# Linear attention on one core: loading V directly into a block layout, with a 128-row first matmul

## Chip, cores, metric

One core of one Trainium2 chip. The metric is device time in microseconds (us) of one execution; most kernels were run several times, and the median is quoted. "Span" is the length of the profiled execution as the trace has it; the measured time is some 1.8 us longer than the span of the same run. Lower is better.

## The reference

```python
batch, heads, seq, dim = 8, 12, 512, 64          # Q, K, V: float32
Q_feat = np.maximum(0, Q) + 1
K_feat = np.maximum(0, K) + 1
KV = np.einsum('bhkd,bhkv->bhdv', K_feat, V)
K_sum = np.sum(K_feat, axis=2)
numerator   = np.einsum('bhqd,bhdv->bhqv', Q_feat, KV)
denominator = np.einsum('bhqd,bhd->bhq', Q_feat, K_sum)
return numerator / (denominator[:, :, :, None] + 1e-10)
```

There are 96 independent heads. Q, K, V and the result are 12.58 MB each. The kernels work in bf16 inside; the loads convert on the way.

## The kernel before

The 96 heads are worked off in 12 groups of 8 heads. A tile has 128 partitions; 32 partitions hold the rows of one head, and the index `n` of 2 picks one of two sets of four heads. So a group has four row blocks `b` of 32 partitions. Loads run four groups ahead (`IN_BUFS`), stores follow three groups behind (`LAG`).

```python
IN_BUFS = 4; OUT_BUFS = 7; LAG = 3
...
def load(g):
    ...
    (nc.sync if first else nc.gpsimd).dma_start(out=k_raw, in_=k_dram[:, g*2 : g*2+2])
    nc.gpsimd.dma_start(out=v_raw, in_=v_dram[:, g*2 : g*2+2])
    nc.gpsimd.dma_start(out=q_raw, in_=q_dram[:, g*2 : g*2+2])

def features(g):                       # max(x + 1, 1) on VectorE; V is copied beside a column of ones
    for half in range(2):
        feature(kf[...], k_raw[...])
        nc.scalar.copy(out=va[:, cs]...[:, :, :, 0:D], in_=v_raw[:, :, cs])     # L110
    ...                                # qf likewise
def kv_and_transpose(g):
    for c in range(16):
        for b in range(4):             # four row tiles of 32 rows, 130 columns each
            nc.tensor.matmul(kva_ps[b//2][:, b%2, 0:130],                       # L126
                lhsT=kf[32*b:32*b+32, c], rhs=va[32*b:32*b+32, c], ...)
    ...                                # PSUM -> kva (ScalarE), transposes of qf, copies to qt (ScalarE)
def output(g):                         # o = qt x kva, then divide by the last column (VectorE)
    ...
for g in range(NG - 1):
    features(g)
    if g >= 1: kv_and_transpose(g - 1)
    if g >= 2: output(g - 2)
    if g + IN_BUFS < NG: load(g + IN_BUFS)
    if g >= LAG: store(g - LAG)
...                                    # the last two groups, then the last four stores
```

All stores but the last go out from GpSimd; the last group's is cut in two halves, issued by SyncE.

## Time and profile before

| | before |
|---|---|
| time, median of 4 runs | 128.02 us (127.78 to 128.51) |
| span of the profiled run | 126.5 us |
| busy share: TensorE, VectorE, ScalarE | 53%, 45%, 51% |
| busy share of the 16 DMA engines, inner slices | 90% or more in each |
| transfers that GpSimd issues | 46 |

No compute engine is busy for much over half of the span, while the DMA engines never rest between the first and the last 3 us. The prediction shows the lines and reads them.

One more view is used in this text. The trace marks, for each transfer, the moments at which each of the 16 DMA engines had finished its share. "First" below is the first of these 16 marks, "last" the last; the transfer counts as landed at the last. Where all engines slip by the same time, both move; where one engine falls behind, only the last moves.

### The profile page before, as it was taken

The page shows a single profiled execution, that of the slowest core. Times are in us where ns is not written, and L with a number is a line of the kernel's source. Part 1 is how long each engine was busy: PE and PEld are TensorE (multiplying, and loading weights), DVE is VectorE, ACT ScalarE, POOL GpSimd, SP SyncE. Part 2 cuts the span into 40 slices and gives each one's busy share as a digit, 9 for nine tenths or more (in the row PEclk, how much of TensorE's full clock was granted, in tenths as well). Part 3 has the DMA queues.
Part 4 walks back from the last instruction along what each step waited for, and adds up shares of the span by engine and source line. Part 5 has one row for each costly group of instructions (what it writes and reads, how often), then busy time and mean ns, then how long its engine had stood idle before and what let it go on. Part 6 is the DMA issues. An engine that isn't in the chain of part 4 may idle for free.

```text
span 126.5 us, 3107 instructions
## 1 busy us (share of the span) xinstructions
PE 67.4 (53%) x1344; PEld 54.8 (43%) x1344; DVE 57.3 (45%) x144; ACT 64.1 (51%) x97; POOL 35.2 (28%) x56
## 2 busy tenths in 40 slices
PE   0009139147949486674648547737916972674000
PEld 0009028036838275562537435626714851563000
DVE  0122222058292865919377067147229079805500
ACT  4041095393966939397590492293096592073000
POOL 6992233222332242233223322332221202010000
PEclk9999999999995958679985555555555577569555
DMA  3999999999999999999999999999999999999990
GB/s 75 340 211 208 212 211 213 208 212 210 214 208 211 212 209 214 209 215 208 251 336 212 229 358 209 212 365 214 210 338 249 215 306 418 420 422 405 409 356 33
DMA packets 13341, 32.17 MB, mean 254 GB/s; under 512 B 784, under 2 KB 784, under 8 KB 13328
## 3 DMA queue, kind: packets, MB, share of 16 engines
q0 software_dynamic: 12512, 29.89, 99.9%
q1 hardware_dynamic: 816, 2.10, 4.6%
q8 instruction: 10, 0.16, 0.5%
q14 instruction: 3, 0.02, 0.0%
HBM read 37.75 MB, written 12.58 MB: 398 GB/s over the span
## 4 chain that ended last, share of the span: by engine, by line
DMA 61%; DVE 13%; PE 8%; POOL 5%; issue 3%; ACT 2%; ACTq 1%; POOLq 0%; DVEq 0%
DMA q_raw<-in_Q_dram 46%; DMA v_raw<-in_V_dram 15%; DVE o_sb L170 9%; PE kva_ps L126 5%; PE qt_ps L146 2%; DVE recip L169 2%; DVE qf L98 2%; POOL v_raw L84 1%; POOL q_raw L85 1%; ACT qt L147 1%; POOL k_raw L81 1%; ACTq L232 1%; ACT v_aug L110 1%; PE o_ps L159 1%; POOL kva_diag L186 1%
## 5 line engine op out<-in xcount | busy, mean ns | idle before, releaser
L110 ACT COPY v_aug<-v_raw 128x1024 bf16<-128x1024 bf16 x24 | 24.1, 1056 | 40.5 <-DMA v_raw<-in_V_dram 40.4
L159 PE MATMUL o_ps<-kva_diag,qt 128*64 128x130 bf16 x384 | 22.9, 269 | 26.7 <-ACT kva_diag L137 15.9
L126 PE MATMUL kva_ps<-v_aug,kf 32*128 32x130 bf16 x768 | 24.6, 294 | 22.8 <-ACT v_aug L110 13.0
L170 DVE TENSOR_TENSOR o_sb<-o_ps,recip 128x512 f32<-128x512 f32 x48 | 33.2, 691 | 1.7
L126 PEld LDWEIGHTS <-kf 32*128 32x128 bf16 x768 | 19.7, 132 | 26.9 <-issue 14.6
L159 PEld LDWEIGHTS <-qt 128*64 128x64 bf16 x384 | 16.6, 137 | 32.7 <-issue 19.1
L147 ACT COPY qt<-qt_ps 128x1024 bf16<-128x1024 bf16 x24 | 29.5, 1298 | 0.5
L98 DVE TENSOR_SCALAR qf<-q_raw 128x1024 bf16<-128x1024 bf16 x24 | 9.4, 434 | 39.0 <-DMA q_raw<-in_Q_dram 39.0
L146 PE MATMUL qt_ps<-identity,qf 128*128 128x128 bf16 x192 | 21.4, 301 | 0.0
L146 PEld LDWEIGHTS <-qf 128*128 128x128 bf16 x192 | 18.5, 140 | 2.3 <-issue 2.0
L92 POOL DMA_DIRECT2D out_dram<-o_sb x11 | 8.4, 767 | 27.9 <-DVE o_sb L170 13.6
L98 DVE TENSOR_SCALAR kf<-k_raw 128x1024 bf16<-128x1024 bf16 (+1 forms) x24 | 9.7, 446 | 12.2 <-DMA k_raw<-in_K_dram 12.2
L137 ACT CAST kva_diag<-kva_ps 64x130 bf16<-64x130 f32 x48 | 10.2, 262 | 9.1 <-PE kva_ps L126 8.8
L169 DVE RECIPROCAL recip<-o_ps 128x8 f32<-128x8 f32 x48 | 9.5, 197 | 8.7 <-PE o_ps L159 8.7
L84 POOL DMA_DIRECT2D v_raw<-in_V_dram x12 | 8.7, 726 | 16.8 <-ACT kva_diag L137 7.3
L85 POOL DMA_DIRECT2D q_raw<-in_Q_dram x12 | 8.6, 720 | 15.8 <-DMA q_raw<-in_Q_dram 5.3
L81 POOL DMA_DIRECT2D k_raw<-in_K_dram x11 | 7.9, 714 | 15.4 <-DMA v_raw<-in_V_dram 8.2
L110 ACT ACT_TABLE_LOAD x1 | 1.3, 1283 | 0.7 <-PEq L221 0.7
L186 POOL MEMSET kva_diag<- 128x520 bf16 x2 | 1.0, 528 | 0.0
L188 POOL MEMSET v_aug<- 128x32 bf16 x2 | 0.4, 278 | 0.0
masks.py:199 POOL TENSOR_SCALAR_AFFINE_SELECT identity<-identity 128x128 bf16<-128x128 bf16 x1 | 0.3, 288 | 0.1
masks.py:197 POOL MEMSET identity<- 128x128 bf16 x1 | 0.2, 232 | 0.0
(4 smaller groups left out, 0.4 us busy)
## 6 DMA issues: line engine op xcount, KB each, us to landing
out_dram<-o_sb POOLq DMA_DIRECT2D x11, 1024.0 KB, 19.9
v_raw<-in_V_dram POOLq DMA_DIRECT2D x12, 512.0 KB, 19.4
q_raw<-in_Q_dram POOLq DMA_DIRECT2D x12, 512.0 KB, 19.4
k_raw<-in_K_dram POOLq DMA_DIRECT2D x11, 512.0 KB, 19.4
k_raw<-in_K_dram SPq DMA_DIRECT2D x1, 1024.0 KB, 4.9
out_dram<-o_sb SPq DMA_DIRECT2D x2, 512.0 KB, 6.9
```

Source lines behind the costliest of these rows:

```text
L81: (nc.sync if first else nc.gpsimd).dma_start(out=k_raw, in_=k_dram[:, g * 2 : g * 2 + 2])
L84: nc.gpsimd.dma_start(out=v_raw, in_=v_dram[:, g * 2 : g * 2 + 2])
L85: nc.gpsimd.dma_start(out=q_raw, in_=q_dram[:, g * 2 : g * 2 + 2])
L98: nc.vector.tensor_scalar(out=dst, in0=src, scalar1=1.0, scalar2=1.0, op0=ALU.add, op1=ALU.max)
L110: nc.scalar.copy(out=va[:, cs].rearrange("p c (n x) -> p n c x", n=2)[:, :, :, 0:D], in_=v_raw[:, :, cs],)
L126: nc.tensor.matmul(kva_ps[b // 2][:, b % 2, 0:W], lhsT=kf[ps, c, :, :], rhs=va[ps, c, :], start=(c == 0), stop=(c == C2 - 1),)
L137: nc.scalar.copy(out=kva[ps, 2 * h : 2 * h + 2, n, :], in_=kva_ps[h][ps, :, D1 * n : D1 * n + D1],)
L146: nc.tensor.transpose(qt_ps[:, c, :], qf[:, half * C + c, :, :], identity)
L147: nc.scalar.copy(out=qt[:, :, :, half], in_=qt_ps)
L159: nc.tensor.matmul(ops[c // 4][64 * j : 64 * j + 64, c // 2 % 2, (c % 2) * W : (c % 2) * W + W], lhsT=qt[:, c, 32 * b : 32 * b + 32, :], r ...
L169: nc.vector.reciprocal(out=recip, in_=cells[:, :, :, :, D:D1])
L170: nc.vector.tensor_tensor(out=o_sb[:, h:NP:2, 4 * i : 4 * i + 4].rearrange("p n (b c) d -> p b c n d", b=2), in0=cells[:, :, :, :, 0:D], i ...
```

## The change

Intent: take the copy of V off ScalarE and use the full height of the array in the first matmul. V is loaded straight into a tile with five blocks per partition; a partition's V goes into the block of its own head, the other three head blocks stay zero, and the fifth holds ones that give the sum of K. One matmul over 128 rows then serves four heads. As the block depends on the partition, a load of V becomes four loads of 32 partitions. The buffers are zeroed once by VectorE. The program order changes too: loads run three groups ahead instead of four, and the first matmul of a group follows directly on the output of two groups earlier. It gets two PSUM buffers of its own, and the pool shared before goes from three buffers to two.

```diff
-OUT_BUFS = 7
+OUT_BUFS = 6
+AHEAD = 3
...
-    v_aug = [const.tile([P, C2, W], BF16, ...) for i in range(2)]
+    v_blk = [const.tile([P, 5, 2, C2, D], BF16, ...) for i in range(3)]
...  load(g)
-        nc.gpsimd.dma_start(out=v_raw, in_=v_dram[:, g * 2 : g * 2 + 2])
-        nc.gpsimd.dma_start(out=q_raw, in_=q_dram[:, g * 2 : g * 2 + 2])
+        if first: (load q_raw here)
+        for b in range(4):
+            nc.gpsimd.dma_start(
+                out=v_blk[g % NV][32 * b : 32 * b + 32, b],
+                in_=v_dram[32 * b : 32 * b + 32, 2 * g : 2 * g + 2])
+        if not first: (load q_raw here)
...  features(g): the ScalarE copy of V is gone
...  first matmul
-        for c in range(C2):
-            for b in range(4):
-                nc.tensor.matmul(kva_ps[b // 2][:, b % 2, 0:W], lhsT=kf[ps, c], rhs=va[ps, c, :], ...)
+        for c in range(C2):
+            for n in range(2):
+                nc.tensor.matmul(kva_ps[64 * n : 64 * n + 64],
+                    lhsT=kf[:, c, n, :], rhs=vb[:, :, n, c, :], ...)      # 320 columns
...  start of the program
+        nc.vector.memset(ones, 0.0)
+        for t in v_blk:    nc.vector.memset(t, 0.0)
+        for t in kva_diag: nc.vector.memset(t, 0.0)
...  main loop
-        for g in range(IN_BUFS): load(g)
+        for g in range(AHEAD): load(g)
...
-            if g >= 1: kv_and_transpose(g - 1)
+            if g >= 1: transposes(g - 1)
             if g >= 2: output(g - 2)
-            if g + IN_BUFS < NG: load(g + IN_BUFS)
+            keys_values(g)
+            if g + AHEAD < NG: load(g + AHEAD)
```

## The prediction

> **What bounds the kernel now.** I read the page first for the DMA row, then the DMA queues, then the waits, then the timelines of the engines around the last load and at the end.
>
> ```profile
> DMA  3999999999999999999999999999999999999990
> GB/s 75 340 211 208 212 211 213 208 212 210 214 208 211 212 209 214 209 215 208 251 336 212 229 358 209 212 365 214 210 338 249 215 306 418 420 422 405 409 356 33
> ...
> q0 software_dynamic: 12512, 29.89, 99.9%
> ...
> HBM read 37.75 MB, written 12.58 MB: 398 GB/s over the span
> ```
>
> The 16 DMA engines are busy in every slice from the second to the last but one. The byte row counts what is written: 211 GB/s where bf16 copies of fp32 inputs land (so 422 GB/s read), 420 GB/s where fp32 results leave. One load of 1.05 MB and one store of 1.05 MB therefore cost the same 2.5 us. Twelve groups have 3 loads and 1 store each: 48 x 2.5 = 120 us of the 126.5 us span. That is the bound.
>
> ```profile
> ACT v_aug L110 <- DMA v_raw<-in_V_dram: 40.4, 11, 6.1
> DVE qf L98 <- DMA q_raw<-in_Q_dram: 39.0, 11, 5.2
> ...
> POOL k_raw L81 <- DMA v_raw<-in_V_dram: 8.2, 4, 2.8
> ```
>
> The waits agree: ScalarE and VectorE wait for loads. The third line shows the other side of the queue: GpSimd issues a transfer only when an earlier one has landed, because eight completion counters are used in turn. So at most eight GpSimd transfers are under way; at 2.5 us each that is the 19.4 us from issue to landing in the issue table.
>
> ```profile
> 94.20 0.76 DVE L98 TENSOR_SCALAR qf<-q_raw 128x1024 bf16<-128x1024 bf16 x2 [4.23 <-DMA q_raw<-in_Q_dram]
> ...
> 101.89 0.21 DVE L169 RECIPROCAL recip<-o_ps 128x8 f32<-128x8 f32 x1 [3.57 <-PE o_ps L159]
> ...
> 105.25 0.75 DVE L98 TENSOR_SCALAR kf<-k_raw 128x1024 bf16<-128x1024 bf16 x2
> ```
>
> The end: the Q of group 10 lands at 94.2. Until the Q of group 11 there are one store and three loads, 10.0 us, so the last load lands near 104.2. VectorE is then still at the output of group 9 and starts the last features at 105.25.
>
> ```profile
> 109.51 1.91 PE L126 MATMUL kva_ps<-v_aug,kf 32*128 32x130 bf16 x62 [0.46 <-DVE o_sb L170]
> 111.36 1.88 PE L146 MATMUL qt_ps<-identity,qf 128*128 128x128 bf16 x16
> ...
> 118.15 0.69 DVE L170 TENSOR_TENSOR o_sb<-o_ps,recip 128x512 f32<-128x512 f32 x1
> ```
>
> The last result is done at 118.84, 14.6 us after the last load. Eight stores (groups 4 to 11) stand behind that load: 20 us of transfers. So the end too is set by DMA, and compute has about 20 + 1.3 - 14.6 - 3.2 = 3.5 us to spare (3.2 us: a half store alone, below; 1.3 us: the last landing, 118.87 + 6.7, less 124.2).
>
> **What the Trainium skill says.**
> (1) "VectorE: DVE Perf Modes", section "Zero memsets can be issued as uint32 (trn2)": a memset takes a cycle per element whatever the type, so zeros go as 4-byte words; its clock is 0.96 GHz. No VectorE memset is in this trace; on GpSimd 520 bf16 elements took 528 ns, also about one per ns.
> (2) "SBUF — State Buffer", section "Door 1: The DMA port swizzle": 32 neighbouring partitions reach only 8 of 16 ports, asymptote about 218 GB/s. No transfer before is so narrow. The bf16 loads write 211 GB/s, just under that.
> (3) "TensorEngine Tiling (Array Packing)", section "Key Properties": tiles of the array load and multiply in parallel. The trace agrees: 8 matmuls of 130 columns on alternate column halves took 0.42 us at granted clock 1.00; eight in a row would need 0.43 us and the pipeline's delay on top, and 24 took 0.87 us, 36 ns each.
> (4) "DMA: Bandwidth & Descriptors", section "Anatomy of one DMA": about 2.0 us fixed plus bytes over 436 GB/s. A half store of 0.52 MB alone: 3.2 us, an estimate. Only queued stores are in the trace (6.7 us).
>
> **The change, part by part.**
> *ScalarE copies of V* go: 24 x 1056 ns, 24.1 us busy. They waited for V (40.4 us), so they lie beside the transfers and give nothing except a shorter step from V to its matmuls.
>
> *First matmul.* Before, 64 matmuls of 130 columns per group, four row tiles at once, 1.91 us. After, 32 of 320 columns in pairs on two column halves: 16 x 320 = 5120 columns, 2.1 us at granted clock 1.00 and 4.3 us at 0.50. TensorE per group at half clock: 4.3 + 1.9 (transposes) + 4 x 0.64 (outputs) = 8.8 us, still below the 10 us of DMA per group. In the steady part this is hidden. The order of instructions shows that V of group g+3 waits for the matmuls of g in the same buffer, but also for a completion counter held by K of g+2. In queue order that K lands 15 us after Q of g (store, three loads, store, load). Features 0.8, the output's TensorE part about 3.5 and 4.3 us are 9 us. So this new wait ends first.
>
> *V loads.* Each group has one load fewer of 256 packets and four more of 64: 36 more transfers in all. Bytes are the same. Two costs. First, each transfer's end: at 435 GB/s 1.05 MB would take 2.41 us and I see 2.5, so an end costs at most 0.09 us; I take 0.03 x 36 = 1.1 us. Second, ports: the V blocks want 211 GB/s of 218, so they just fit; I put 0 in the centre, but 15% on 12 x 2.5 = 30 us of V would be 4.5 us. GpSimd issues six or seven per group at up to 0.72 us, 5 us of 10. The eight in flight are now 7 transfers per 4.2 MB, about 11 us of work instead of 20; the queue doesn't run dry.
>
> *Head.* Before, V waits for nothing. After, it waits for VectorE to zero its block: 5120 words / 0.96 GHz = 5.3 us from 0.8, so V of group 0 is issued from 6.2 to about 9, the other blocks are free at 11.6 and 17.0. K and Q of group 0 keep the DMA busy until about 8. The V blocks follow at one per 0.7 us against 0.62 us of transfer each; then the identity (0.6 us) delays K of group 1 to 9.7, landing flow near 11.0 against 9.9. One bubble of about 1.0 us. The later blocks are zeroed in time. VectorE's features of group 0 start near 19.7 instead of 5.7, and the first matmuls end near 25; V of group 3 isn't due before 28. That hides.
>
> *Tail.* AHEAD of 3 puts store 4 before load 11, so the last load lands 2.5 us later and 7 stores (17.5 us) follow instead of 8. The sum of transfers is the same, but compute's spare falls by 2.5 us to 1.0. The first matmul of group 11 lies fully on the compute path, and that of group 10 lies before the output of group 9 on TensorE. At granted clock 1.00 they add 0.2 us and little; at 0.50 they add 2.4 and about 2.1 us (the own PSUM pool gives a little back). Of 4.5 us, 3.6 stick out past DMA. The clock in 111.4 to 113.3 was 0.56 and in 114.9 to 115.8 it was 1.00, so I take +1.5 us.
>
> Sum: 126.5 + 1.0 (head) + 1.1 (transfer ends) + 1.5 (tail) = 130.1 us of span. The time runs 1.56 us above the span (128.06 - 126.5): 131.6 us, +2.8%.
>
> **The rivals.**
> *A, same time.* DMA stays the bound, ends are free, TensorE's clock is full at the end: 126.5 + 0.3 to 1.0 gives 128.4 to 129.1. For: no group's bound changes. Against: the head bubble and the shorter spare at the end.
> *B, narrow V loads are port bound.* Each V group takes 15 to 30% longer: +4.5 to 9 us, 134 to 138. For: 211 of 218 leaves no room for uneven arrival. Against: even blocks are followed by odd ones and engines drift apart, which mixes ports.
> *C, faster.* ScalarE's freed 24 us would have to be on the path. Against: the DMA row has no gap to give back. 120 us of transfers, start and landing of about 5 us and 1.56 make 126.5 at best; I see no way to 125.5.
>
> **Range and chances.** Low end: A, 128.5. High end: my sum with a third to half of B and the whole tail, 135.5. 2% is 130.6. My centre is 1 us above it; A's share and a full clock at the end leave much below. Faster 0.02, same 0.38, slower 0.60.
>
> **What would show it.** Right: ScalarE's V copy gone and no gain from it; VectorE memsets of 5.3 us each at the start; V of group 0 issued near 6.2; a dip in the DMA row in the third or fourth slice; first matmuls 2 to 4 us per group; a last result later against the last load than 14.6 us, with DMA not at its full rate just before the last store. Wrong: V loads landing with over 0.7 us each between them (B); a memset far from 5.3 us; a hole in the DMA row in mid-kernel, where GpSimd waits for TensorE; last stores back to back (then no tail cost, A).

## The result

The changed kernel is correct and slower: 132.84 us median of 4 runs (131.37 to 133.53; one of the four in the slow state), before 128.02. The ratio is 1.0345, 95% interval 1.0268 to 1.0422. Ratios here and below are the mean time of one kernel's fast runs over that of the kernel before's fast runs of the same rounds, so not quite the ratio of the medians.

From the page of the changed kernel, the rows that answer to those of before: DMA share in tenths by slice, bytes written by slice, the GpSimd queue, HBM totals.

```profile
DMA  4998999999999999999999999999999999999944
GB/s 100 321 155 137 149 202 200 206 211 208 210 210 210 212 206 211 208 237 344 212 228 346 215 220 351 220 215 349 227 210 343 237 208 351 424 411 419 368 169 179
...
q0 software_dynamic: 13088, 29.89, 98.3%
...
HBM read 37.75 MB, written 12.58 MB: 385 GB/s over the span
```

Bytes and middle are as before: 200 to 212 GB/s in each slice with loads alone. Two stretches are not. The third to fifth slices (6.5 to 16.3 us) carry 155, 137 and 149 GB/s where the kernel before carries 211, 208 and 212, and the last two are at four tenths, where the kernel before was at nine in the last but one and had finished in the last.

The head on GpSimd, from its timeline (start, length, line, what; in brackets the idle time before it and what ended it):

```profile
1.27 0.83 POOL L89 DMA_DIRECT2D q_raw<-in_Q_dram  x1 [0.82 <-POOLq L234]
6.54 2.13 POOL L91 DMA_DIRECT2D v_blk<-in_V_dram  x4 [4.45 <-DVE v_blk L186]
...
9.21 0.72 POOL L85 DMA_DIRECT2D k_raw<-in_K_dram  x1
11.87 2.12 POOL L91 DMA_DIRECT2D v_blk<-in_V_dram  x4 [1.95 <-DVE v_blk L186]
```

GpSimd sits for 4.45 us and then 1.95 us until VectorE has zeroed a V buffer. The zeroing starts every 5.34 us (first two of three rows):

```profile
1.91 4.33 DVE L186 MEMSET v_blk<- 128x5120 uint32 x1 [1.04 <-issue]
...
7.25 4.33 DVE L186 MEMSET v_blk<- 128x5120 uint32 x1 [1.01 <-issue]
```

What that does to the transfers shows in stretches of 1 us. The columns are the stretch, its length, busy time of the five compute rows, granted clock (the share of its full clock that TensorE was granted), DMA share, and GB/s written. The changed kernel:

```profile
7.00:8.00 1.00, 0.00 (x0) 0.00 (x0) 0.75 (x1) 0.00 (x0) 1.00 (x3) 1.00 0.81 115
8.00:9.00 1.00, 0.00 (x0) 0.00 (x0) 1.00 (x1) 0.00 (x0) 0.93 (x4) 1.00 0.80 145
9.00:10.00 1.00, 0.00 (x0) 0.00 (x0) 1.00 (x1) 0.00 (x0) 0.92 (x2) 1.00 1.05 182
...
11.00:12.00 1.00, 0.00 (x0) 0.00 (x0) 0.57 (x1) 0.00 (x0) 0.13 (x1) 1.00 0.53 66
12.00:13.00 1.00, 0.00 (x0) 0.00 (x0) 0.41 (x1) 0.00 (x0) 1.00 (x3) 1.00 1.01 135
13.00:14.00 1.00, 0.00 (x0) 0.00 (x0) 1.00 (x1) 0.00 (x0) 1.00 (x3) 1.00 1.17 150
14.00:15.00 1.00, 0.00 (x0) 0.00 (x0) 1.00 (x1) 0.00 (x0) 1.00 (x2) 1.00 0.78 131
```

In the same stretches the kernel before has 203 to 217 GB/s. By the landing marks, the V blocks of group 0 finish between 9.22 and 11.54 us and K of group 1, a full load, between 13.87 and 16.76; the first V block of group 1 has its first mark only at 15.86. So the low rate from 12 to 15 us is mostly that of K.

The end, from TensorE's and VectorE's timelines of the changed kernel:

```profile
115.14 4.14 PE L130 MATMUL kva_ps<-v_blk,kf 128*64 128x320 bf16 x32
...
119.22 1.07 PE L149 MATMUL qt_ps<-identity,qf 128*128 128x128 bf16 x16
...
126.26 0.69 DVE L173 TENSOR_TENSOR o_sb<-o_ps,recip 128x512 f32<-128x512 f32 x1
```

The first matmul of the last group takes 4.14 us instead of 1.91, the last result is done at 126.95, and DMA stands still just before it:

```profile
124.00:125.00 1.00, 0.51 (x8) 0.40 (x8) 0.97 (x3) 0.00 (x0) 0.00 (x0) 0.50 0.28 115
125.00:126.00 1.00, 0.77 (x12) 0.40 (x8) 0.97 (x3) 0.00 (x0) 0.00 (x0) 0.50 0.00 0
```

The landing marks tell how much was lost where. Times are us from the start of the span; "Q 2" is the Q load of group 2, "stretch" the time from the last mark of Q 10 to the last result. GpSimd runs a long DRAIN instruction after its last issue; "drain over" is the end of it.

| kernel | Q 2 first | Q 10 first / last | last result | stretch | last GpSimd store landed | GpSimd drain over | last SyncE store landed | span |
|---|---|---|---|---|---|---|---|---|
| before | 25.31 | 92.48 / 94.18 | 118.84 | 24.7 | 123.85 | 125.78 | 125.59 | 126.5 |
| changed | 28.03 | 98.13 / 100.27 | 126.95 | 26.7 | 125.38 | 128.78 | 129.71 | 130.6 |

Up to Q 2 both kernels have moved the same loads, so the head costs 28.03 - 25.31 = 2.7 us. From Q 2 to Q 10 the changed kernel takes 70.10 us and the kernel before 67.17; one more store (2.5 us) lies in it by the new order, so the middle costs 0.4 us. The stretch of compute after Q 10 grew by 2.0 us. Of the 4.1 us by which the span grew, head and middle leave 0.9 for the end.

### The profile page after: what moved, and what is told of

It reads as the page before. It is cut to its first block, busy times and chain, and to the rows that moved or that the text cites. A ratio compares the mean times of both kernels' runs of the same rounds, so it can differ in the third digit from the quotient of the medians.

```text
span 130.6 us, 2367 instructions
## 1 busy us (share of the span) xinstructions
PE 71.8 (55%) x960; PEld 52.2 (40%) x960; DVE 72.4 (55%) x158; ACT 41.2 (32%) x73; POOL 51.9 (40%) x88
## 4 chain that ended last, share of the span: by engine, by line
DMA 43%; DVE 29%; PE 11%; issue 6%; POOL 5%; ACT 2%; ACTq 1%; POOLq 0%
DMA q_raw<-in_Q_dram 34%; DVE o_sb L173 10%; DVE v_blk L186 10%; DMA k_raw<-in_K_dram 9%; PE kva_ps L130 8%; POOL v_blk L91 5%; DVE qf L109 3%; DVE recip L172 2%; PE o_ps L162 2%; DVE kf L109 2%; DVE kva_diag L188 1%; ACT qt L150 1%; ACTq L245 1%; PE qt_ps L149 1%; DVE v_blk L196 0%
## 5 line engine op out<-in xcount | busy, mean ns | idle before, releaser
L130 PE MATMUL kva_ps<-v_blk,kf 128*64 128x320 bf16 x384 | 40.7, 383 | 20.1 <-DVE kf L109 20.1
L162 PE MATMUL o_ps<-kva_diag,qt 128*64 128x130 bf16 x384 | 21.1, 251 | 34.0 <-DVE o_sb L173 31.0
L91 POOL DMA_DIRECT2D v_blk<-in_V_dram x48 | 26.3, 555 | 33.8 <-DMA k_raw<-in_K_dram 11.3
L130 PEld LDWEIGHTS <-kf 128*64 128x64 bf16 x384 | 27.4, 143 | 29.7 <-DVE kf L109 20.5
L162 PEld LDWEIGHTS <-qt 128*64 128x64 bf16 x384 | 14.0, 124 | 40.0 <-DVE o_sb L173 35.6
L140 ACT CAST kva_diag<-kva_ps 64x256 bf16<-64x256 f32 x24 | 8.9, 371 | 63.7 <-PE kva_ps L130 63.4
L186 DVE MEMSET v_blk<- 128x5120 uint32 x3 | 13.0, 4325 | 3.1 <-issue 3.1
L149 PE MATMUL qt_ps<-identity,qf 128*128 128x128 bf16 x192 | 13.4, 226 | 0.0
L149 PEld LDWEIGHTS <-qf 128*128 128x128 bf16 x192 | 11.4, 101 | 3.8 <-issue 3.8
L141 ACT CAST kva_diag<-kva_ps 64x4 bf16<-64x4 f32 x24 | 4.1, 169 | 0.0
## 6 DMA issues: line engine op xcount, KB each, us to landing
v_blk<-in_V_dram POOLq DMA_DIRECT2D x48, 128.0 KB, 9.3
```

What stands on the lines that cost most here:

```text
L91: nc.gpsimd.dma_start(out=v_blk[g % NV][32 * b : 32 * b + 32, b], in_=v_dram[32 * b : 32 * b + 32, 2 * g : 2 * g + 2],)
L130: nc.tensor.matmul(kva_ps[64 * n : 64 * n + 64], lhsT=kf[:, c, n, :], rhs=vb[:, :, n, c, :], start=(c == 0), stop=(c == C2 - 1),)
L140: nc.scalar.copy(out=kva[ps, :, n, 0:D], in_=kva_ps[ps, 0:4, :])
L149: nc.tensor.transpose(qt_ps[:, c, :], qf[:, half * C + c, :, :], identity)
L162: nc.tensor.matmul(ops[c // 4][64 * j : 64 * j + 64, c // 2 % 2, (c % 2) * W : (c % 2) * W + W], lhsT=qt[:, c, 32 * b : 32 * b + 32, :], r ...
L186: nc.vector.memset(t, 0.0)
```

## The experiments

Eleven kernels were run in three calls, each with runs of the kernel before beside it. The medians of before were 127.89, 128.10 and 128.27 us in the three calls. The changed kernel was not run again beside them: experiments on it are compared with it by ratio, and its interval (1.0268 to 1.0422, three fast runs) is wide.

### e1_fill_first: other loads ahead of the waiting V

```diff
  load(0): K, Q                      load(1): K, Q
+ then V of group 0, V of group 1    (was: V right after each group's K or Q)
```

> Changed kernel, but K and Q of group 1 are issued before the first V blocks, so that work stands in the DMA queue while VectorE zeroes the V buffers. Theory (head): the 3.2 us of DMA that the changed kernel lost between 7 and 21 us come from V waiting for the zeroing with nothing queued behind it; they should come back, about 129.3 us, and the DMA byte rate in 7 to 21 us should be near 211 GB/s throughout. Rival (the V blocks are slow by their narrowness): the rate still falls to about 150 GB/s where V blocks land and the time stays within 1 us of the changed kernel.

Measured: 130.57 us (6 runs, 129.52 to 131.31), ratio 1.0196 (1.0155 to 1.0237) instead of 1.0345. The byte rate in three of the same stretches:

```profile
8.00:9.00 1.00, 0.00 (x0) 0.00 (x0) 1.00 (x1) 0.00 (x0) 0.65 (x2) 1.00 1.10 209
11.00:12.00 1.00, 0.00 (x0) 0.00 (x0) 0.57 (x1) 0.00 (x0) 0.13 (x1) 1.00 1.18 223
12.00:13.00 1.00, 0.00 (x0) 0.00 (x0) 0.41 (x1) 0.00 (x0) 1.00 (x3) 1.00 1.08 201
```

The first mark of Q 2 is at 25.34, that of the kernel before is at 25.31: the head is fully restored, with the zeroing untouched. Its cost was transfers waiting with nothing queued behind them, not the zeroing itself. Of the 2.7 us, 1.5% (1.9 us) came out as time, short of the 3 us expected, as the end then waits longer for compute: the last result is at 125.87, and DMA stands still from 123 to 125 us.

### e2_lag4: every store one group later

```diff
-OUT_BUFS = 6
-LAG = 3
+OUT_BUFS = 7
+LAG = 4
```

> Changed kernel with LAG 4 instead of 3 and OUT_BUFS 7 instead of 6: every store is issued a group later, so that 8 stores stand behind the last load as before the change. Theory (tail): the hole of 2 to 3 us in the DMA row just before the last two stores closes and the time falls by 0.5 to 1.5 us, to about 131.2, and varies less between runs. Rival (the end is plain DMA time): same time within 0.3 us.

Measured: 131.70 us (6 runs, 130.61 to 132.22), ratio 1.0277 (1.0238 to 1.0315). The gain has the expected size, but the interval overlaps that of the changed kernel, so this run alone does not show it; e5_both below does. The mechanism was not as expected: the hole did not close.

```profile
124.00:125.00 1.00, 0.81 (x16) 0.56 (x12) 0.97 (x3) 0.00 (x0) 0.00 (x0) 0.50 0.16 66
```

The loads come 2.5 us earlier against the stores, so the first mark of Q 10 is at 95.25, but its last mark is at 98.73 (two engines come 1.5 us after the other 14 in this run) and compute still needs 27.5 us from there. In this profile the last SyncE store has landed at 129.04 and the program still ends only at 130.5, because GpSimd's drain is over at 129.68. That drew attention to the drain.

### e3_before_narrow: four V loads in the kernel before

```diff
-        nc.gpsimd.dma_start(out=v_raw, in_=v_dram[:, g*2 : g*2+2])
+        for b in range(4):
+            nc.gpsimd.dma_start(out=v_raw[32*b : 32*b+32],
+                in_=v_dram[32*b : 32*b+32, g*2 : g*2+2])
```

> Kernel before, with only the V load cut into four of 32 partitions into the same tile: no zeroing, no new matmul, no new order. Theory: with other work in the queue narrow loads cost next to nothing, 0 to +1.1 us (36 more transfer ends), about 128.5 us. Rival (port bound): +4.5 us or more, 132.5 or above, and a byte rate that falls by 15% or more through the load phase.

Measured: 130.21 us (6 runs, 129.27 to 131.02), ratio 1.0167. Neither theory: the time grew by 2.1 us, but the transfers hardly slowed down. Q 10 has its first mark at 92.96 against 92.48, so 0.5 us for eleven groups of narrow loads and what surrounds them, and the last SyncE store landed at 126.24 against 125.59. The program, however, ended 2.5 us after that landing instead of 0.95. The difference is on GpSimd. The rows of its drains at the program's end (lengths in ns least/median/most, then first and last start in us), first the kernel before:

```profile
L232 POOLq DRAIN  x3: 51/102/15211, 110.6 to 126.3; - x3
```

Then e3_before_narrow:

```profile
L236 POOLq DRAIN  x3: 51/108/17206, 110.8 to 128.5; - x3
```

The longest drain begins when GpSimd has issued its last store. It ends at 110.6 + 15.2 = 125.8 before and at 110.8 + 17.2 = 128.0 here; the last GpSimd stores landed at 123.85 and 124.58. So it goes on for 1.93 and 3.40 us after the last landing. It is 3.40 us in all profiles with 82 GpSimd transfers (changed kernel, e1, e2, e3, e4, e5, e9), whatever else differs.

### e4_even_odd: another order of the four V blocks

```diff
-        for b in range(4):
+        for b in (0, 2, 1, 3):
```

> Changed kernel, with the four V blocks of a group loaded in the order 0, 2, 1, 3 instead of 0, 1, 2, 3, so that blocks of the lower and the upper 64 partitions alternate. If the low rate in 12 to 15 us (131 to 150 GB/s with only V blocks queued) comes from eight SBUF ports shared by all engines, [...]that stretch should rise towards 200, worth 0.5 to 1 us in all, about 131.8 us. If it comes from the start of each small transfer (one issue per 0.53 us, few in flight), nothing changes.

Measured: 132.47 us (6 runs, 131.31 to 134.50, one slow), ratio 1.0331. The stretch that the expectation names:

```profile
12.00:13.00 1.00, 0.00 (x0) 0.00 (x0) 0.41 (x1) 0.00 (x0) 1.00 (x3) 1.00 0.84 135
13.00:14.00 1.00, 0.00 (x0) 0.00 (x0) 1.00 (x1) 0.00 (x0) 1.00 (x3) 1.00 1.07 162
14.00:15.00 1.00, 0.00 (x0) 0.00 (x0) 1.00 (x1) 0.00 (x0) 1.00 (x2) 1.00 1.04 115
```

No rise, no gain. But as shown above, what lands in this stretch is mostly K of group 1, which the edit does not touch. The V blocks of group 0 land before it:

```profile
9.00:10.00 1.00, 0.00 (x0) 0.00 (x0) 1.00 (x1) 0.00 (x0) 0.92 (x2) 1.00 1.01 162
10.00:11.00 1.00, 0.00 (x0) 0.00 (x0) 1.00 (x1) 0.00 (x0) 0.00 (x0) 1.00 1.03 162
```

The changed kernel has 182 and 199 there, so they did not gain either. Alternating the halves of the partitions does nothing here, and shared ports as the cause of these stretches are not supported. That they are slow because small transfers start on a nearly empty queue is not shown: K is no small transfer. What makes it slow stays open, except that it does not happen with work queued ahead (e1_fill_first).

### e9_short_matmul: the first matmul made short

```diff
-                    kva_ps[64*n : 64*n+64],        rhs=vb[:, :,   n, c, :]     # 320 columns
+                    kva_ps[64*n : 64*n+64, 3:5],   rhs=vb[:, 3:5, n, c, :]     # 128 columns
-            in_=kva_ps[ps, 0:4, :]
+            in_=kva_ps[ps, 3:4, :].to_broadcast([64, 4, D])
```

> Changed kernel, wrong result on purpose: the first matmul streams only two of its five column blocks (128 columns instead of 320), and the copies out of PSUM read one block four times. Theory (tail): from the landing of the Q of group 10 to the last result took 26.65 us in the changed kernel against 24.6 before, because the first matmuls of groups 10 and 11 take 3.3 and 4.1 us; here they take at most 1.8 us each and that stretch should fall to about 23 us, so the hole before the last stores closes. The drain then binds (last GpSimd store landed near 125.4, plus 3.4 and 0.75): span near 129.5, time near 131.3, about 1 us less than the changed kernel. Rival (first matmul is hidden): no change.

Measured: the result is wrong, as intended; 131.27 us (6 runs, 130.38 to 131.73), ratio 1.0248 (1.0213 to 1.0282) instead of 1.0345. The stretch from Q 10 to the last result fell from 26.7 to 23.2 us, and the hole closed:

```profile
123.00:124.00 1.00, 0.00 (x0) 0.00 (x0) 0.60 (x1) 0.00 (x0) 0.00 (x0) 0.50 1.03 418
124.00:125.00 1.00, 0.00 (x0) 0.00 (x0) 0.00 (x0) 0.00 (x0) 0.00 (x0) 0.50 1.00 393
125.00:126.00 1.00, 0.00 (x0) 0.00 (x0) 0.00 (x0) 0.00 (x0) 0.00 (x0) 0.50 1.03 397
```

The longer first matmul thus costs about 1.0% of the time (1.2 us) in the changed kernel; the two intervals overlap slightly, so that size is rough. The stretch shrank by 3.5 us: below that the end is held by other things, here the drain (over at 128.93; the last SyncE store had landed at 128.07).

### e10_before_ahead3: the order alone

```diff
-        for g in range(IN_BUFS): load(g)              # IN_BUFS = 4
+        for g in range(AHEAD): load(g)                # AHEAD = 3
-            if g + IN_BUFS < NG: load(g + IN_BUFS)
+            if g + AHEAD < NG: load(g + AHEAD)
```

> Kernel before with three groups of loads issued ahead instead of four, nothing else: store 4 then stands before the last load and 7 stores behind it, as in the changed kernel. Theory: compute in the kernel before has 3.5 us to spare at the end and loses 2.5 of them, so the time stays within 0.5 us of 128.1; only with the longer first matmul does the shorter spare show. Rival (the order alone costs the tail): 129 or more.

Measured: 127.71 us (22 runs, 127.54 to 128.47), ratio 0.9959 (0.9942 to 0.9975). Fewer loads ahead cost nothing in the kernel before. It is the fastest kernel of this study, but by 0.4% only.

### e5_both and e6_both_sp: the repairs together

e5_both is the changed kernel with the edits of e1_fill_first and e2_lag4. e6_both_sp adds:

```diff
-            nc.gpsimd.dma_start(out=o_to, in_=o_sb)
+            eng = nc.sync if g >= NG - 4 else nc.gpsimd
+            eng.dma_start(out=o_to, in_=o_sb)
```

> Changed kernel with both earlier edits: K and Q of group 1 ahead of the first V blocks, and LAG 4. New theory, from the last stretch of all traces so far: GpSimd's drain at the program's end finishes 3.40 us after its last store has landed wherever GpSimd issued 82 transfers (1.93 us after, with 46), and can end later than the last SyncE store. By it this version is bound by the drain: last GpSimd store landed near 123.5, drain over near 126.9, span near 127.7, time near 129.3. Rival (only compute after the last loads counts): 27 us from the landing of the Q of group 10 near 95.6, last store landed near 125.6, span near 126.5, time near 128.2.

> As e5_both, with the stores of groups 8, 9 and 10 issued from SyncE instead of GpSimd, so that GpSimd's last transfer lands some 8 us before the end. Drain theory: the drain no longer ends the program; 0.7 to 1.2 us less than e5_both, near 128.4, which would equal the kernel before. Rival (the drain merely waits for the program's last transfer): no difference from e5_both.

Measured: e5_both 129.00 us (6 runs, 128.65 to 129.88), ratio 1.0093 (1.0056 to 1.0130); e6_both_sp 129.31 us (7 runs, 128.24 to 129.54), ratio 1.0085 (1.0052 to 1.0118). The two repairs take the changed kernel from 3.5% to 0.9% above the kernel before, and e5_both against e1_fill_first (1.0155 to 1.0237) shows that the later stores gain 1.0% once the head is filled. In e5_both the drain does end the program, as the first theory said: over at 126.12, when the last SyncE store had landed at 125.24. In e6_both_sp the drain is over at 125.93, before the last SyncE store, so it no longer ends the program; but that store landed at 126.66, 1.4 us later than in e5_both, and the time is the same. The last mark of its Q 10 was already 1.1 us later before any of the moved stores, and a moved store of group 8 overtook older ones of GpSimd (landed at 113.05, ahead of stores issued before it). Which of the two used up the gain is not settled; as a test of the drain this run is inconclusive.

### e7_narrow_sp: the drain taken off the end of e3

e3_before_narrow with the same edit of the stores as in e6_both_sp.

> Kernel before with V in four narrow loads (e3_before_narrow, 130.2) and with the stores of groups 8, 9 and 10 issued from SyncE. Drain theory: of the 2.2 us that the four loads cost there, 1.5 us were the longer drain and go away: near 128.7. Rival (the four loads slow the transfers themselves): still near 130.2.

Measured: 129.11 us (6 runs, 128.52 to 129.30), ratio 1.0076 instead of 1.0167. So 0.9% (1.2 us) of the cost of the four loads was the drain, which is now over at 125.50 while the last SyncE store lands at 126.28. The remaining 0.8% is left to the transfers and their landing (the last SyncE store lands 0.7 us later than in the kernel before).

### e8_before_halves and e11_before_v_q_quarters: does the drain go by the number of transfers?

e8 is e3_before_narrow with V in two loads of 64 partitions; e11 has V and Q in four each.

> Kernel before with V in two loads of 64 partitions: GpSimd issues 58 transfers instead of 46. The drains read so far (1.93 us after the last GpSimd store's landing at 46 transfers, 3.27 at 79, 3.40 at 82) lie on 0.05 + 0.041 x transfers: expected 2.43 us here, and about 0.6 to 0.8 us more time than the kernel before. Rival (the drain depends on the narrow V loads themselves, not on the count): 1.93 or 3.40 us.

> Kernel before with V and Q each in four loads of 32 partitions: GpSimd issues 118 transfers. Drain by the line: 4.89 us after the last GpSimd store's landing, so a span near 130.3 and a time near 132. Rival (the drain has a ceiling or depends on V's loads): 3.4 us and a time near 130.5. The time while loads run should grow by less than 1.5 us even with eight quarter loads in flight (5 us of work).

Measured: e8_before_halves 128.99 us (18 runs, 127.91 to 129.77), ratio 1.0048 (1.0023 to 1.0074). Its drain row:

```profile
L236 POOLq DRAIN  x3: 51/102/15632, 110.4 to 126.6; - x3
```

It is over at 126.08, 2.42 us after the last GpSimd store's landing at 123.66; 2.43 was expected. With 1.93 us at 46 transfers, 2.42 at 58, 3.28 at 79 and 3.40 at 82, these lie on a line of 41 ns per transfer.

e11_before_v_q_quarters missed: 118 transfers, yet the drain was over 0.38 us after the last GpSimd landing, where 4.89 was expected. The kernel took 134.13 us in its one fast run (the profiled one, 136.87, was in the slow state). GpSimd issued its last store at 122.72, though the result that it needed was ready at 119.75 and its timeline names no wait for the 6.88 us of idle time before it. The work may have been done there instead of at the end; no run shows it. The line holds from 46 to 82 transfers and is not to be carried beyond that.

The other half of that expectation, that the loads lose less than 1.5 us, missed too. In the profiled slow run the last quarter of Q of group 10 has its first mark at 100.66 against 92.48, 8.2 us later, and GpSimd waits 25.2 us in all until a load of K has landed before it issues the next Q quarter (eight of its transfers are under way at most, and six to eight of them are now quarters). The fast run, which has no profile, was still 5.9 us slower than the kernel before. Whether narrowness, the shorter queue or the slow state takes the 8.2 us is open.

## Why the prediction held, step by step

**The bound and ScalarE: right.** The transfers remain the bound, and the copies of V went (ScalarE busy 41.2 us instead of 64.1) without bringing any time.

**The middle: right, with one term too large.** The new first matmul took 2.34 us at granted clock 1.00, 4.14 at 0.56 and 4.48 at 0.50 (start 73.14); the prediction's 2.1 and 4.3 come from 2.4 columns per ns, a rate that it gives no source for, and 5120 columns in 2.34 us are 2.2. The byte rate between 22 and 98 us is as before. I took 1.1 us for the ends of 36 more transfers; 0.4 us (changed kernel) and 0.5 us (e3_before_narrow) were measured.

**The head: right mechanism, size wrong by a factor of almost three.** The prediction put "One bubble of about 1.0 us"; it was 2.7 us, and e1_fill_first shows it by giving all of it back. The issue times were right within 0.5 us (6.54 for 6.2, 9.21 for 9.7, 11.87 for 11.6). The step that failed is that there would be one bubble, before K of group 1. Against 211 GB/s the rates fall short by 0.7 us of transfers from 11 to 12 us, where the prediction had it, but also by 0.9 us from 7 to 10 and by 1.4 us from 12 to 17. The first of these was not foreseen: the first V block, issued at 6.54, has its first mark at 9.22, 1.45 us after that of Q of group 0 (7.77), where 0.64 is the pace of V blocks. The last stands where the prediction says "The later blocks are zeroed in time": K of group 1 finishes between 13.87 and 16.76, and behind it come the V blocks of group 1, which waited for their zeroing until 11.87, with a first mark at 15.86. How much of this is K's slow landing and how much the late V blocks is not separated by any run; e1_fill_first removes both.

**The tail: right.** I predicted 1.5 us beyond DMA from the first matmul at a clock between half and full. The stretch after Q 10 grew by 2.0 us, and taking the longer matmul away gave 1.2 us. One reading was off: it put the landing of the last load near 104.2, and the marks of Q of group 11 run from 102.43 to 105.18. That the shorter spare by the order of loads does no harm alone is shown by e10_before_ahead3.

**What the prediction didn't have: the drain.** From 46 to 82 transfers, each GpSimd transfer adds 41 ns to the drain at the program's end. In the changed kernel's profiled run this hides behind the last SyncE store (128.78 against 129.71), but it limits what repairs of the tail can bring, and it is most of what the four V loads cost in the kernel before.

**The rivals.** B, ports: against it speak e3 (0.5 us of transfers where 4.5 or more were claimed) and e4, which alternates the lower and the upper 64 partitions. That even blocks after odd ones mix ports, the prediction's own reason against B, no run shows. B's 134 to 138 is also not the sum of its parts: 128.1 + 4.5 to 9 is 132.6 to 137.1. A, same time: the head bubble and the tail that I set against it were both real. C, faster: nothing of it.

**Sum.** Predicted 130.1 us of span; the profiled run has 130.6, the other fast runs 129.6 and 131.5. So the total is right partly by luck: a head 1.7 us too small stood beside transfer ends 0.7 us and an end 0.6 us too large (0.9 for 1.5). The end was as small as 0.9 us for a reason that the prediction lacks. In the kernel before, the last SyncE store lands 3.1 us after its first mark (two engines come last), in the changed one, where the queue had run dry, 0.2 us after; by first marks (122.53 and 129.53) the end lost 3.9 us. The 1.56 us that the prediction adds to the span compares different runs: the profiled run of the kernel before took 128.40 us, 1.9 above its span, so the centre should have been near 131.9. **Open:** why some DMA engines fall behind (Q 10 in e2_lag4: two of 16), what slowed K of group 1 in the head, and what GpSimd does in its drain.

## What to carry to other kernels

Here DMA was the bound, freeing a compute engine brought nothing, and the change was paid for at both ends of the program. In such a case, look for what makes a first transfer wait, and put other transfers ahead of it; look at which compute lies between the last load and the last store, and count it at the low clock. Cutting V alone into four cost the loads 0.5 us while the queue was full, but with Q cut as well (e11) the fast run was 5.9 us slower. Each further transfer from GpSimd may also be paid again when the program ends, so compare the last landing with the end of the span.

## What the Trainium skill lacked or had wrong

- No page says that GpSimd's drain at the program's end outlasts its last store, and the longer the more it has issued: 1.93 us after the last GpSimd store's landing with 46 transfers, 2.42 with 58, 3.28 with 79, 3.40 with 82; 0.38 with 118 (belongs to "DMA: Bandwidth & Descriptors").
- "SBUF — State Buffer", "Door 1: The DMA port swizzle", gives 32 partitions 8 of 16 ports, about 218 GB/s. Here converting loads write 211 GB/s, and up to Q 10 44 narrow loads in place of 11 full ones cost about 0.5 us while the queue was full; an order that alternates partition halves changed nothing. The page speaks of two narrow transfers at a time, not of narrow loads among full ones in a long queue.
- "DMA: Bandwidth & Descriptors", "Anatomy of one DMA": its fit, made for GpSimd's transfers, gave an estimate of 3.2 us for a half store alone; from SyncE the trace has 2.7 us from issue to the last mark (125.30 to 128.04).
- "VectorE: DVE Perf Modes", "Zero memsets can be issued as uint32 (trn2)": agrees, 5.34 us from start to start against 5120 / 0.96 GHz = 5.33. The profile's row says 4.33 us, with 1.0 us before it as "issue", so the row alone seems to understate it; the page doesn't say so.
